# A 31-tap depthwise convolution split into even and odd tokens, with a new list schedule around it

## The chip, the core and the metric

The kernel runs on one core of one Trainium2 chip. The metric is the time of one execution of the program in microseconds (us) on the device. A second, profiled execution gives the trace that is read here; its span is the stretch from the first to the last instruction that the profiler records.

PE is TensorE (matmuls; PEld its weight loads), DVE is VectorE, ACT is ScalarE, POOL is GpSimd and SP is SyncE. POOL and SP do almost nothing here but issue transfers.

## What is computed

One layer of a hybrid decoder on 512 tokens of 1024 channels, in fp32. Cut to what matters:

```python
h = rmsnorm(x); proj = h @ w_in          # gb, gc, v | u, ug | q | three gates
y_a = (gb * conv3(gc * v)) @ w_a_out
u = u * sigmoid(ug)
u = causal_dwconv(u, conv_b_w) + conv_b_bias          # 31 taps, per channel
y_b = silu(layernorm(u)) @ w_b_out
y_c = cross_attention(q, mem) @ w_att_out
merged = sum(sigmoid(gate_i) * y_i)
x = x + merged @ w_o
x = x + (silu(conv3(h2 @ w_up)[gate]) * conv3(h2 @ w_up)[value]) @ w_down
out = rmsnorm(x)

def causal_dwconv(x, w):   # y[t] = sum_k w[k] * x[t - K + 1 + k]
```

The change touches the 31-tap convolution, `causal_dwconv(u, conv_b_w)`.

## The kernel before, in words

**Matmuls.** Every large product is taken in blocks ("quads") by a seven-product scheme of the Strassen kind, and each of the seven products is done three times, on a high and a low part of both operands (`multiply`, the matmuls of L681). One product of one quad, such as `(("mq", 1), 2)`, is 24 matmuls. Its weights come in as one 128x1024 tile from HBM; ACT casts the high part (`whi`, job `wh`, L500), DVE subtracts to get the low part (`wlo`, job `wl`, L504). For some products the low part is instead made by a negated copy on ACT (job `wn`, L519) and an accumulating transfer issued by POOL (L521). There are four buffers for such pairs, so a cast may run at most four products ahead of PE. Between a quad's products, partial sums are read from PSUM by ACT (jobs `r1`, `r5`, `r6`, `r4`: L708, L712, L723, L731) and DVE (`r2`, `r7`, `r3`: L457, L715).

**Stages by time.** PE does keys and values (to 60 us), the projections of `w_in` and the attention (60 to 440), the first output products (`merge`), the last gate, branch B's output product (quads `mq 0` and `mq 1`, 515 to 553), the merged product with `w_o` (stages `wo a` to `wo g`, 553 to 597), the up projection (597 to 835, eleven pairs of quads `up 0` to `up 10`), and the down projection to the end. The activations' combinations for branch B's quads (named `b00`, `b10`, `b11`, `t4` to `t7` after the seven products) are split into high (L1386, ACT) and low parts (L1391, DVE).

**The 31-tap convolution** (L1206 to L1267) runs on ACT and DVE alone. For each of four pairs `p` of 128-channel tiles (one 128x1024 tile: two tiles of 512 tokens) ACT writes the first product with the bias into a new tile `acc` (L1221, twice 128x512). Of the other 30 shifts, 23 are done as a product on ACT into a temporary `tp` (L1246, two instructions of 128 x (512 - s)) and an addition of both halves on DVE (L1253, one instruction); the seven shifts that are multiples of four are done on DVE alone by a multiply-add (L1238, two instructions). The four results are then summed and centred for the layer norm (`tot1`, `tot2`, `centre`, `lns`), and a swish is taken (L1344).

**Order.** PE's order is written out by hand (`QUAD_ORDER`, `WO`, `UP`, `DOWN`). Everything else is a job of class `Jobs` (L122 to L333): each job has an engine, an estimated cost, its predecessors and the tiles that it takes. The due time of a job is worked back from the PE product that needs it; then the scheduler repeatedly takes the job that can start first, and among those the one that is due first. Two tables bend this: `LATER` adds an offset to the due time of a kind of job, and `AHEAD` keeps a kind from starting more than so many us before it is due. `issue_in_program_order` then holds every engine to the order found, so an instruction that waits holds up all that stand behind it on its engine. Tiles live in rings (17 + 6 large places, 6 load buffers, 6 temporaries, 8 PSUM banks); a load waits until its place is free. The planner charges a fixed table cost to ACT only at the first sigmoid (`sg 0`), the exponentials, one later sigmoid and the first silu; the swish (L1344) and the second half of the gate's sigmoid (L1511) carry no such cost.

Of the kernel before, what the change touches and what calls it, by code (L numbers as in the profile page):

```python
# [10 lines left out]
AF = mybir.ActivationFunctionType  # L11
# [5 lines left out]
KC = D // P  # L17
# [54 lines left out]
LATER = {  # L72
    "ACT cf": 96, "ACT high": -211, "ACT kh": 28, "ACT oh": -43, "ACT qh": -31, "ACT r1 mq": -254,
# [3 lines left out]
    "DVE h2 t4": -36, "DVE kl": -6, "DVE kt": 11, "DVE mgl a": 32, "DVE mgl f": 25,  # L77
    "DVE ms d": 104, "DVE ptl": 21, "DVE ql": 99, "DVE r2 gate": 78, "DVE r2 up": 14,
    "DVE s6 glu": -67, "DVE tap 3": -4, "DVE tot1": -33, "DVE vl": 158, "DVE weigh": 139,
# [5 lines left out]
}  # L85

AHEAD = {
# [3 lines left out]
}  # L91


# [243 lines left out]
def hybrid_block_kernel(  # L337
# [64 lines left out]
    def two(key):  # L402

        return tiles[key].rearrange("p (c n) -> p c n", c=2)
# [34 lines left out]
    def par(key, i):  # L439
        return pk[:, cols[key] + i : cols[key] + i + 1]  # L440
# [544 lines left out]
    for p in range(4):  # L985
# [35 lines left out]
            use=[("x", p), ("rows", "x")] + (hb if p % 2 else []))  # L1021

    job(("ldp",), "SP", 0.3, lambda: nc.sync.dma_start(
        out=pk[:, N_GAINS:], in_=packed[:, N_GAINS:]), [("ldx", 3)], LOAD_LATENCY)
    scale_jobs("x", R_X, ("ss", "x"), NT)

    def pe_squares(s, key, n, width, after, total=1024):
# [175 lines left out]
               use=[("pth", h), ("ptl", h), ("vh", h // 2), ("vl", h // 2)], unit=False)  # L1203


    def by_act(p, s):  # L1206

        return s in ACT_TAPS

    for p in range(4):  # L1210
        job(("sg", p), "ACT", actv(1024) + (0 if p else TABLE), lambda p=p: nc.scalar.activation(
            tiles["ug", p], tiles["ug", p], AF.Sigmoid), ready_of(("glu", p), 0),
            use=[("ug", p)])
        job(("um", p), "DVE", dve(1024), lambda p=p: nc.vector.tensor_tensor(
            tiles["u", p], tiles["u", p], tiles["ug", p], op=ALU.mult),
            [("sg", p)] + ready_of(("glu", p), 1), use=[("ug", p), ("u", p)])

        def conv_start(p=p):
            make(("acc", p))
            for j in range(2):  # L1220
                nc.scalar.activation(  # L1221
                    two(("acc", p))[:, j, :], two(("u", p))[:, j, :], AF.Identity,
                    bias=par("conv_b_bias", 2 * p + j),
                    scale=par("conv_b_w", (K_B - 1) * KC + 2 * p + j),
                )

        job(("tap", p, 0), "ACT", 2 * scaled_act(512, 0.09), conv_start,
            [("um", p), ("ldp",)] + ([("tap", p - 1, K_B - 4)] if p else []),
            take=[(("acc", p), ANY)], use=[("u", p)])
        made_taps = []  # L1230
        for s in range(1, K_B):
            def weight(j, p=p, s=s):
                return par("conv_b_w", (K_B - 1 - s) * KC + 2 * p + j)

            def tap(p=p, s=s, weight=weight):
                for j in range(2):
                    a = two(("acc", p))[:, j, s:]
                    nc.vector.scalar_tensor_tensor(  # L1238
                        a, two(("u", p))[:, j, : SEQ - s], weight(j), a,
                        op0=ALU.mult, op1=ALU.add,  # L1240
                    )

            def tap_product(p=p, s=s, weight=weight):
                make(("tp", p, s))
                for j in range(2):
                    nc.scalar.activation(  # L1246
                        two(("tp", p, s))[:, j, s:], two(("u", p))[:, j, : SEQ - s], AF.Copy,
                        scale=weight(j),
                    )

            def tap_add(p=p, s=s):
                a = two(("acc", p))[:, :, s:]
                nc.vector.tensor_tensor(a, a, two(("tp", p, s))[:, :, s:], op=ALU.add)  # L1253

            if by_act(p, s):
                job(("tp", p, s), "ACT", 2 * scaled_act(512 - s), tap_product,
                    [("tap", p, 0), ("ldp",)] + made_taps[-2:-1], take=[(("tp", p, s), ANY)],
                    use=[("u", p)])
                job(("tap", p, s), "DVE", dve(1024 - 2 * s), tap_add,
                    [("tap", p, s - 1), ("tp", p, s)], use=[("acc", p), ("tp", p, s)])  # L1260
                made_taps.append(("tap", p, s))
            else:
                job(("tap", p, s), "DVE", 2 * TAP, tap, [("tap", p, s - 1), ("ldp",)],
                    use=[("acc", p), ("u", p)])


    conv_done = [("tap", p, K_B - 1) for p in range(4)]  # L1267

    def first_sum(key, a, b):
        make(key)  # L1270
# [6 lines left out]
    def sums_split(s, key):  # L1277
# [12 lines left out]
            use=[key])  # L1290
        job((s, "low"), "DVE", dve(512), low, [(s, "high")], use=[key, (s, "parts")])

    job("tot1", "DVE", dve(1024), lambda: first_sum(("tot",), ("acc", 0), ("acc", 1)),
        conv_done[:3], take=[(("tot",), ANY)], use=[("acc", 0), ("acc", 1)])
    job("tot2", "DVE", dve(1024), lambda: add_into(("tot",), ("acc", 2)), ["tot1", conv_done[2]],
        use=[("tot",), ("acc", 2)])
    job(("mu", "sum"), "DVE", dve(1024), lambda: add_into(("tot",), ("acc", 3)),
        ["tot2", conv_done[3]], use=[("tot",), ("acc", 3)])
    sums_split("mu", ("tot",))

    def channel_mean(s):
# [10 lines left out]
        return t.unsqueeze(1).broadcast_to([P, 2, SEQ])  # L1312

    for p in range(4):
        acc = ("acc", p)
        job(("centre", p), "DVE", dve(1024), lambda p=p: nc.vector.tensor_tensor(
            two(("acc", p)), two(("acc", p)), on_both(tiles["bank", "mu"]), op=ALU.subtract),
            [("mu", "mean")], use=[acc, ("bank", "mu")])

        def centre_square(p=p):  # L1320
            make(("csq", p))
            nc.scalar.activation(tiles["csq", p], tiles["acc", p], AF.Square)
# [10 lines left out]
    scale_jobs("v", R_V, ("ss", "v"), NT)  # L1333

    for p in range(4):
        acc = ("acc", p)
        job(("lns", p), "DVE", dve(1024), lambda p=p: nc.vector.tensor_tensor(
            two(("acc", p)), two(("acc", p)), on_both(tiles["rows", "v"]), op=ALU.mult),
            [("v", "rows")], use=[acc, ("rows", "v")])

        def swish(p=p):
            for j in range(2):
                t = two(("acc", p))[:, j, :]
# [22 lines left out]


    def rows_of(p, r):
        return two(("acc", p))[:, :, r * HALF : (r + 1) * HALF]

    def y_parts(key, e, src, after, use):
        last = next(f for f in OPERAND if OPERAND[f] == key)
# [26 lines left out]

    Y5 = ("y", "t5")  # L1400
    for e in range(2):
        top, end = ("acc", e), ("acc", 2 + e)
# [434 lines left out]
    for q in range(QUADS):  # L1837
# [5 lines left out]
        for value, src, acc in ((0, ("gt", q), ("gtc", q)), (1, ("uu", q), ("upc", q))):  # L1843
            conv3_jobs(
                ("cf", q, value), src, acc,
                lambda k, j, q=q, v=value: par(
                    "conv_ffn_w", k * 2 * FC + v * FC + 2 * q + j),
                ready_of(up, value) + ([("z", q - 1)] if q else []), "tm",
            )
        job(("silu", q), "ACT", actv(1024) + (0 if q else TABLE), lambda q=q: nc.scalar.activation(  # L1850
            tiles["gtc", q], tiles["gtc", q], AF.Silu), [(("cf", q, 0), "done")],
# [484 lines left out]
```

## Time and profile before

| | |
|---|---|
| median of 3 runs | 929.57 us (927.53 to 930.92) |
| profiled execution | 929.3 us, of it span 927.5 us |
| granted TensorE clock, mean | 0.997 |
| PE busy | 914.6 us (99%) |
| DVE busy | 852.0 us (92%) in 980 instructions |
| ACT busy | 685.2 us (74%) in 938 instructions |
| transfers | 196.91 MB, 212 GB/s on the mean |

A row of a view reads: line, engine, operation, output <- inputs, shapes, count, then busy time and mean length. An instruction's length overlaps a little with the next one's: neighbours of 128x1024 on DVE are 1.22 us long and start 1.14 us apart, on ACT 1.05 long and 0.95 apart. A row of waits reads: engine, line <- what it waited for: us in all, times, longest.

### The profile page before, as it was taken

The page shows a single profiled execution, that of the slowest core. Times are in us where ns is not written, and L with a number is a line of the kernel's source. Part 1 is how long each engine was busy: PE and PEld are TensorE (multiplying, and loading weights), DVE is VectorE, ACT ScalarE, POOL GpSimd, SP SyncE. Part 2 cuts the span into 40 slices and gives each one's busy share as a digit, 9 for nine tenths or more (in the row PEclk, how much of TensorE's full clock was granted, in tenths as well). Part 3 has the DMA queues.
Part 4 walks back from the last instruction along what each step waited for, and adds up shares of the span by engine and source line. Part 5 has one row for each costly group of instructions (what it writes and reads, how often), then busy time and mean ns, then how long its engine had stood idle before and what let it go on. Part 6 is the DMA issues. An engine that isn't in the chain of part 4 may idle for free.

```text
span 927.5 us, 17130 instructions
## 1 busy us (share of the span) xinstructions
PE 914.6 (99%) x6821; PEld 866.5 (93%) x6821; DVE 852.0 (92%) x980; ACT 685.2 (74%) x938; POOL 137.1 (15%) x165
## 2 busy tenths in 40 slices
PE   9999999999999999999999998999999999999997
PEld 8999999999989999999899996898999999988886
DVE  6897999999999999799996999996989889999977
ACT  7576988889997886678857973875766676765655
POOL 0021111100011211110110211121121121002300
PEclk9999999999999999999999999999999999999999
DMA  9999788745679888897857899999999677789972
GB/s 358 394 262 204 176 162 182 180 115 111 172 155 267 181 186 178 198 238 202 204 131 189 209 287 322 231 218 301 253 236 230 152 171 169 188 271 314 264 139 91
DMA packets 56097, 196.91 MB, mean 212 GB/s; under 512 B 6353, under 2 KB 6737, under 8 KB 56017
## 3 DMA queue, kind: packets, MB, share of 16 engines
q0 software_dynamic: 22608, 81.54, 48.9%
q1 hardware_dynamic: 33120, 114.02, 34.1%
q8 instruction: 53, 0.87, 0.4%
q10 hardware_dynamic: 288, 0.27, 0.1%
q14 instruction: 28, 0.22, 0.1%
HBM read 191.60 MB, written 4.19 MB: 211 GB/s over the span
## 4 chain that ended last, share of the span: by engine, by line
PE 91%; DVE 5%; DMA 3%; issue 1%; ACT 0%; SPq 0%; DVEq 0%; POOL 0%; POOLq 0%; ACTq 0%
PE bank L681 60%; PE bank L453 6%; PE bank L452 6%; PE bank L451 6%; PE bank L1486 3%; PE bank L1488 3%; PE bank L1487 3%; PE bank L937 2%; DMA ('up', 3)_966_7341<-in_w_up 2%; DVE wlo L504 1%; DMA y_sum<-in_w_down 1%; DVE mg L1562 1%; DVE mgl L1672 1%; PE bank L1864 0%; PE ss L810 0%
## 5 line engine op out<-in xcount | busy, mean ns | idle before, releaser
L500 ACT CAST whi<-wf 128x1024 fp32r<-128x1024 f32 x206 | 214.8, 1044 | 102.0 <-PE bank L681 53.5
L504 DVE TENSOR_TENSOR wlo<-wf,whi 128x1024 fp32r<-128x1024 f32 (+1 forms) x200 | 241.6, 1212 | 31.4 <-ACT whi L500 28.4
L1246 ACT ACTIVATE tp<-u,pk 128x482 f32<-128x482 f32 (+22 forms) x184 | 118.9, 704 | 4.2 <-DVE acc L1253 3.7
L1253 DVE TENSOR_TENSOR acc<-acc,tp 128x1022 f32<-128x1022 f32 (+22 forms) x92 | 109.2, 1188 | 4.0 <-ACT tp L1246 2.7
L638 POOL DMA_DIRECT2D wf<-in_w_in x50 | 44.2, 891 | 231.8 <-DVE wlo L504 185.7
L681 PE MATMUL bank<-ft6h,whi 128*128 128x256 f32 x248 | 69.4, 280 | 2.4 <-ACT gt L708 2.4
L681 PE MATMUL bank<-ft6h,wlo 128*128 128x256 f32 x248 | 69.4, 280 | 0.0
L681 PE MATMUL bank<-ft6l,whi 128*128 128x256 f32 x248 | 69.4, 280 | 0.0
L681 PE MATMUL bank<-fb11h,wlo 128*128 128x256 f32 x248 | 68.6, 277 | 0.5 <-DVE wlo L504 0.5
L681 PE MATMUL bank<-ft5h,whi 128*128 128x256 f32 x248 | 68.9, 278 | 0.0
L681 PE MATMUL bank<-ft5l,whi 128*128 128x256 f32 x248 | 68.8, 278 | 0.0
L681 PE MATMUL bank<-ft5h,wlo 128*128 128x256 f32 x248 | 68.8, 278 | 0.0
L681 PE MATMUL bank<-fb10h,whi 128*128 128x256 f32 x248 | 68.8, 278 | 0.0
L681 PE MATMUL bank<-fb00h,whi 128*128 128x256 f32 x248 | 68.8, 277 | 0.0
L681 PE MATMUL bank<-ft7h,whi 128*128 128x256 f32 x248 | 68.7, 277 | 0.0
L681 PE MATMUL bank<-ft7l,whi 128*128 128x256 f32 x248 | 68.7, 277 | 0.0
L681 PE MATMUL bank<-ft7h,wlo 128*128 128x256 f32 x248 | 68.7, 277 | 0.0
L681 PE MATMUL bank<-fb00l,whi 128*128 128x256 f32 x248 | 68.7, 277 | 0.0
L681 PE MATMUL bank<-fb00h,wlo 128*128 128x256 f32 x248 | 68.7, 277 | 0.0
L681 PE MATMUL bank<-fb11h,whi 128*128 128x256 f32 x248 | 68.7, 277 | 0.0
L681 PE MATMUL bank<-fb10h,wlo 128*128 128x256 f32 x248 | 68.6, 277 | 0.0
L681 PE MATMUL bank<-fb10l,whi 128*128 128x256 f32 x248 | 68.6, 277 | 0.0
(408 smaller groups left out, 3150.6 us busy)
## 6 DMA issues: line engine op xcount, KB each, us to landing
wf<-in_w_in SPq DMA_DIRECT2D x52, 512.0 KB, 5.3
wf<-in_w_in POOLq DMA_DIRECT2D x50, 512.0 KB, 6.7
wf<-in_w_up SPq DMA_DIRECT2D x31, 512.0 KB, 6.6
wf<-in_w_up POOLq DMA_DIRECT2D x30, 512.0 KB, 7.0
wf<-in_w_down SPq DMA_DIRECT2D x15, 512.0 KB, 4.1
wf<-in_w_att_out SPq DMA_DIRECT2D x8, 512.0 KB, 3.5
wf<-in_w_a_out SPq DMA_DIRECT2D x8, 512.0 KB, 4.5
wf<-in_w_b_out SPq DMA_DIRECT2D x8, 512.0 KB, 5.9
```

Of the source, the lines that this page charges most:

```text
L451: nc.tensor.matmul(ps, s_hi, w_hi, start=start, stop=False, skip_group_check=again)
L452: nc.tensor.matmul(ps, s_hi, w_lo, start=False, stop=False, skip_group_check=again)
L453: nc.tensor.matmul(ps, s_lo, w_hi, start=False, stop=stop, skip_group_check=again)
L500: nc.scalar.copy(parts[0], src())
L504: nc.vector.tensor_tensor(lo, src(), hi.bitcast(F32), op=ALU.subtract)
L638: nc.gpsimd.dma_start(out=tiles[key], in_=block(w, col[c], k), accum_op=ALU.add)
L681: nc.tensor.matmul(ps[:, c, :], w[:, k, at], a[k], start=first and n == 0, stop=i == 3 and n == 2, skip_group_check=again,)
L1246: nc.scalar.activation(two(("tp", p, s))[:, j, s:], two(("u", p))[:, j, : SEQ - s], AF.Copy, scale=weight(j),)
L1253: nc.vector.tensor_tensor(a, a, two(("tp", p, s))[:, :, s:], op=ALU.add)
L1486: nc.tensor.matmul(ps, w_hi[:, i, at], hi, start=first, stop=False)
L1487: nc.tensor.matmul(ps, w_hi[:, i, at], lo, start=False, stop=False)
L1488: nc.tensor.matmul(ps, w_lo[:, i, at], hi, start=False, stop=last)
```

## The change

The convolution is taken on even and odd tokens apart. With a sequence of 256 even and one of 256 odd tokens per tile, a 31-tap filter falls into 16 even and 15 odd taps, which would need four convolutions of half the length (each sort of token with each sort of tap). Three are made: even tokens with even-numbered taps and odd with odd (`ab`, four rows of 256), and the sum of even and odd tokens with the sums of neighbouring taps (`cc`); the last less the first two gives the mixed terms. The tokens are read in place with a step of two elements (`parity`).

- New on DVE: `taps` (sums of taps, once), `xsum2` (sum of even and odd tokens, one 128x512), `less`, `even`, `odd` (putting together, about 128x512 each), with strided reads in `xsum2` and strided writes in `even` and `odd`.
- On ACT, each pair `p` has 4 products to start `ab`, 50 products for its shifts 1 to 15 without 4 and 9, and 32 for `cc`: 86 products of 128 x (256 - s), 54 of them reading with the step of two.
- On DVE, shifts 4 and 9 of `ab` are done by four multiply-adds of 128 x (256 - s) each; the other shifts are 12 additions of 128 x 4 x (256 - s) and one of 128 x 2 x 241; `cc` takes 15 additions of 128 x 2 x (256 - s).
- The result goes back into `u`, so the tile `acc` is gone. The sums of taps take the place of `conv_ffn_w` in the packed parameters, whose load is split off as `ldf` behind `("less", 3)`; the FFN's convolution waits for it.
- `LATER` goes from 57 entries to 9, `AHEAD` from 14 to 4, and with them the order of all jobs on ACT, DVE, SP and POOL is found anew. PE's order is the same, instruction by instruction.

```diff
-ACT_TAPS = [s for s in range(1, 31) if s % 4]
+DVE_TAPS = (4, 9)
...
 LATER = {
-    "ACT cf": 96, "ACT high": -211, "ACT kh": 28, "ACT oh": -43, "ACT qh": -31, "ACT r1 mq": -254,
...
+    "DVE fl h2 t4": 7, "DVE fl h2 t7": 82, "DVE kt": 114, "DVE r7 up": -172, "DVE vl": 43,
+    "DVE wl mix 2": 4, "SP ld merge 0": -11, "SP ld up s": -15, "SP ld up v": -7,
 }
...
+        def parity(j, r, n=HALF, u=u):
+            return two(u)[:, j, r : r + 2 * n - 1 : 2]
+        def x_sum(u=u, cc=cc):
+            make(cc)
+            nc.vector.tensor_tensor(
+                four(cc)[:, 0:2, :], two(u)[:, :, 0::2], two(u)[:, :, 1::2], op=ALU.add)
...
+            def tap_product(s=s, tp=tp, d=d, parity=parity, weight=weight):
+                make(tp)
                 for j in range(2):
-                    nc.scalar.activation(
-                        two(("tp", p, s))[:, j, s:], two(("u", p))[:, j, : SEQ - s], AF.Copy,
-                        scale=weight(j),
-                    )
-            def tap_add(p=p, s=s):
-                a = two(("acc", p))[:, :, s:]
-                nc.vector.tensor_tensor(a, a, two(("tp", p, s))[:, :, s:], op=ALU.add)
+                    for r in range(1 if s == TAPS - 1 else 2):
+                        nc.scalar.activation(
+                            four(tp)[:, 2 * j + r, d:], parity(j, r, HALF - d), AF.Copy,
+                            scale=weight(s, j, r))
+            def tap_add(tp=tp, d=d, rows=rows, ab=ab):
+                a = four(ab)[:, rows, d:]
+                nc.vector.tensor_tensor(a, a, four(tp)[:, rows, d:], op=ALU.add)
...
+        def less_even(cc=cc, ab=ab):
+            c = four(cc)[:, 2:4, :]
+            nc.vector.tensor_tensor(c, c, four(ab)[:, 0::2, :], op=ALU.subtract)
+        def even_tokens(u=u, ab=ab):
+            a, b = four(ab)[:, 0::2, :], four(ab)[:, 1::2, :]
+            nc.vector.tensor_copy(two(u)[:, :, 0:1], a[:, :, 0:1])
+            nc.vector.tensor_tensor(
+                two(u)[:, :, 2::2], a[:, :, 1:], b[:, :, : HALF - 1], op=ALU.add)
+        def odd_tokens(u=u, ab=ab, cc=cc):
+            nc.vector.tensor_tensor(
+                two(u)[:, :, 1::2], four(cc)[:, 2:4, :], four(ab)[:, 1::2, :], op=ALU.subtract)
```

Three places of the new order are shown; line numbers of the changed kernel are its own (its L488 is L500 before, L492 is L504, L507 is L519, L1479 is L1391, L1755 is L1667, L1938 is L1850).

The first is DVE in branch B's quads (about 523 to 531 us of the trace before). A row `wlo` is the low part of a weight tile. Before, `wlo_6189` is that of product 2 of `mq 1`, `wlo_6222` that of product 6 of `mq 0`; `ft7l` and `ft6l` are low parts of branch B's activations:

```order
L1521 TENSOR_TENSOR g_4970<-bank_5896,g_4970 128x512
L504 TENSOR_TENSOR wlo_6189<-wf_5956,whi_6188 128x1024
L1391 TENSOR_TENSOR ft7l_6152<-acc_2344,ft7h_6151 128x512
L504 TENSOR_TENSOR wlo_6222<-wf_5777,whi_6221 128x1024
L457 SCALAR_TENSOR_TENSOR acc_1146<-acc_1146 128x2x256
L457 SCALAR_TENSOR_TENSOR acc_2344<-acc_2344 128x2x256
L457 SCALAR_TENSOR_TENSOR acc_3233<-acc_1146,acc_3233 128x2x256
L504 TENSOR_TENSOR wlo_6264<-wf_5880,whi_6263 128x1024
L1391 TENSOR_TENSOR ft6l_6269<-acc_1146,ft6h_6268 128x512
```

In the changed kernel `wlo_6309` is that of product 2 of `mq 0`, `wlo_6387` that of product 6 of `mq 0`, and `wlo_6351` that of product 2 of `mq 1`:

```order
L445 SCALAR_TENSOR_TENSOR u_757<-u_757 128x2x256
L492 TENSOR_TENSOR wlo_6309<-wf_6092,whi_6308 128x1024
L445 SCALAR_TENSOR_TENSOR u_893<-u_893 128x2x256
L492 TENSOR_TENSOR wlo_6387<-wf_5944,whi_6386 128x1024
L1479 TENSOR_TENSOR ft6l_6393<-u_757,ft6h_6392 128x512
L1479 TENSOR_TENSOR ft6l_6393<-u_893,ft6h_6392 128x512
L492 TENSOR_TENSOR wlo_6351<-wf_6123,whi_6350 128x1024
L492 TENSOR_TENSOR wlo_6436<-wf_6047,whi_6435 128x1024
L703 TENSOR_TENSOR y_6313<-y_6313,bank_6400 128x2x256
```

The low part for product 2 of `mq 1` moved behind that for product 6 of `mq 0` and behind both low parts of `ft6`; PE still takes product 2 of `mq 1` first.

The second is ACT ahead of the stage `wo` (about 541 to 552 us). L519 (L507) is the negated copy after which POOL issues the accumulating transfer; `whoh` and `whol` are the halves of `w_o`'s own tiles, `mgh` is the high part of the merged activations. Before:

```order
L500 CAST whoh_6443<-wf_6339 128x1024
L519 ACTIVATE whol_6444<-wf_6339 128x1024
L500 CAST whi_6476<-wf_5880 128x1024
L500 CAST whoh_6484<-wf_6377 128x1024
L1667 CAST mgh_6489<-mg_6480 128x512
L519 ACTIVATE whol_6485<-wf_6377 128x1024
L500 CAST whoh_6518<-wf_6413 128x1024
L1667 CAST mgh_6527<-mg_6516 128x512
L519 ACTIVATE whol_6519<-wf_6413 128x1024
L500 CAST whoh_6556<-wf_6447 128x1024
L1667 CAST mgh_6489<-mg_6480 128x512
L519 ACTIVATE whol_6557<-wf_6447 128x1024
```

In the changed kernel:

```order
L488 CAST whi_6606<-wf_5944 128x1024
L488 CAST whoh_6611<-wf_6532 128x1024
L507 ACTIVATE whol_6612<-wf_6532 128x1024
L488 CAST whi_6645<-wf_6047 128x1024
L1755 CAST mgh_6650<-mg_6643 128x512
L488 CAST whoh_6655<-wo_6433 128x1024
L488 CAST whoh_6683<-wf_6577 128x1024
L488 CAST whi_6687<-wo_6346 128x1024
L507 ACTIVATE whol_6684<-wf_6577 128x1024
L488 CAST whoh_6723<-wf_6614 128x1024
L1755 CAST mgh_6650<-mg_6643 128x512
L507 ACTIVATE whol_6724<-wf_6614 128x1024
```

Ahead of the second negated copy (`whol_6485` before, `whol_6684` now) stand two more casts, `whoh_6655` and `whi_6687`, of tiles that were cast behind the fourth negated copy before. POOL issues the four transfers in the same order in both.

The third is ACT in the up projection (about 645 to 652 us), around the first silu. L708 (L696) is the first read of quad `up 2` from PSUM, for which PE waits; `whi_7581` (`whi_7744` now) is the cast for product 7 of `up 2`, and L731 (L719) the last read of `up 1`. Before:

```order
L500 CAST whi_7537<-('up', 3)_966_7341 128x1024
L1850 ACT_TABLE_LOAD
L1850 ACTIVATE gtc_7475<-gtc_7475 128x1024
L500 CAST whi_7572<-wf_7236 128x1024
L731 ACTIVATE uu_7408<-bank_7042 128x2x256
L708 COPY gt_7579<-bank_7123 128x2x256
L500 CAST whi_7581<-wf_6937 128x1024
L500 CAST whi_7611<-('up', 3)_977_7439 128x1024
```

In the changed kernel:

```order
L488 CAST whi_7704<-('up', 3)_963_7510 128x1024
L1938 ACT_TABLE_LOAD
L1938 ACTIVATE gtc_7642<-gtc_7642 128x1024
L488 CAST whi_7737<-wf_7435 128x1024
L488 CAST whi_7744<-wf_7147 128x1024
L696 COPY gt_7748<-bank_7302 128x2x256
L719 ACTIVATE uu_7437<-bank_7205 128x2x256
L488 CAST whi_7776<-('up', 3)_974_7610 128x1024
```

The cast for product 7 moved ahead of that first read, and the last read of `up 1` behind it.

More of the change, by code (lines that the diff above doesn't have):

```diff
@@ L1267, in hybrid_block_kernel @@
-    conv_done = [("tap", p, K_B - 1) for p in range(4)]
+        u, ab, cc = ("u", p), ("ab", p), ("cc", p)
+        def parity(j, r, n=HALF, u=u):
[4 more added lines that the diff above has]
+                four(cc)[:, 0:2, :], two(u)[:, :, 0::2], two(u)[:, :, 1::2], op=ALU.add)
+        job(("xsum2", p), "DVE", dve(512), x_sum, [("um", p)] + ([("less", p - 1)] if p else []), take=[(cc, ANY)], use=[u])
@@ new lines, in sums_product, with sums_start @@
+        def sums_product(out, row, i, p=p, cc=cc):
+            for j in range(2):
+                at = (TAPS - 1) * KC + 2 * p + j
+                more = {"bias": tap_sums[:, at : at + 1]} if i == 0 else {}
+                nc.scalar.activation(
+                    four(out)[:, row + j, i:], four(cc)[:, j, : HALF - i],
+                    AF.Copy if i else AF.Identity, scale=sum_of_taps(i, 2 * p + j), **more)
+        def sums_start(cc=cc, sums_product=sums_product):
+            sums_product(cc, 2, 0)
@@ L1269, in first_sum @@
+        job(("less", p), "DVE", dve(512), less_even, [last[cc], last[ab]], use=[cc, ab])
+        job(("even", p), "DVE", dve(512) + 0.1, even_tokens, [last[ab], last[cc]], use=[u, ab])
+        job(("odd", p), "DVE", dve(512), odd_tokens, [("less", p), ("even", p)],
+            use=[u, ab, cc])
+    conv_done = [("odd", p) for p in range(4)]
     def first_sum(key, a, b):
@@ L1342, in swish @@
             for j in range(2):
[L1343 removed]
+                t = two(("u", p))[:, j, :]
                 nc.scalar.activation(
```

143 lines of the change are left out of this document (93 added, 50 removed), and 11 rows, old and new, of tables (AHEAD, LATER).

## The prediction, made before the changed kernel was run

> **What bounds the kernel now.** First the page: busy time of each engine, and the chain that ended last.
>
> ```profile
> PE 914.6 (99%) x6821; PEld 866.5 (93%) x6821; DVE 852.0 (92%) x980; ACT 685.2 (74%) x938; POOL 137.1 (15%) x165
> PE 91%; DVE 5%; DMA 3%; issue 1%; ACT 0%; SPq 0%; DVEq 0%; POOL 0%; POOLq 0%; ACTq 0%
> ```
>
> PE is busy 914.6 of 927.5 us and makes 91% of the chain. Its order is the same after the change, so its own work is a constant, and a gain can come only from its waits. The view of PE's waits lists them all:
>
> ```profile
> PE bank L681 <- ACT gt L708: 2.4, 1, 2.4
> PE bank L452 <- DMA whol<-in_w_o: 2.2, 2, 1.5
> PE bank L1864 <- POOL ident masks.py:199: 1.4, 1, 1.4
> PE bank L681 <- DVE wlo L504: 0.5, 1, 0.5
> PE bank L452 <- DVE wlo L504: 0.4, 1, 0.4
> PE bank L453 <- DVE zl L2028: 0.3, 1, 0.3
> ```
>
> That is 7.2 us, of which the 1.4 at the start stays. None names the convolution (L1221 to L1253). Third, busy time by stretch, to see which engines have room where (stretch; its length; PE, PEld, DVE, ACT, POOL busy; granted clock, DMA share, GB/s):
>
> ```profile
> 100.00:230.00 130.00, 130.00 (x1089) 128.10 (x1088) 126.05 (x160) 114.92 (x186) 16.44 (x19) 1.00 0.71 156
> 230.00:285.00 55.00, 55.00 (x297) 47.63 (x296) 53.66 (x58) 47.69 (x70) 6.07 (x7) 1.00 0.72 178
> 285.00:390.00 105.00, 105.00 (x919) 104.88 (x918) 98.49 (x105) 79.11 (x107) 18.20 (x21) 1.00 0.86 197
> 460.00:508.00 48.00, 48.00 (x325) 44.24 (x324) 40.30 (x43) 30.35 (x39) 4.32 (x5) 1.00 0.73 171
> 508.00:534.00 26.00, 26.00 (x223) 25.65 (x222) 24.94 (x33) 25.29 (x38) 6.96 (x8) 1.00 0.83 190
> 534.00:573.00 39.00, 36.77 (x243) 32.47 (x242) 38.97 (x52) 23.62 (x28) 5.17 (x6) 1.00 1.04 308
> 652.00:654.00 2.00, 2.00 (x12) 2.00 (x11) 2.00 (x3) 1.81 (x4) 0.00 (x0) 0.50 1.11 262
> 654.00:656.00 2.00, 2.00 (x14) 2.00 (x14) 1.97 (x3) 1.36 (x2) 1.75 (x2) 0.71 1.06 229
> ```
>
> From 100 to 390 us, where most of the convolution runs, PE never waits. DVE is the fuller of the two there: 278.20 busy of 290, ACT 241.72. PE first loses time in 534 to 573, when DVE is busy 38.97 of 39 and the DMA engines are full. Between the two lies 460 to 508, where DVE is busy only 40.30 of 48 and PE all the time: whatever lead DVE has won by then ends as idle time, since its next work needs PE's results. The last two rows belong to the wait of 2.4 us near 650: behind it the clock stood at 0.50 and 0.71 for 2 us each, which cost 1.00 + 0.58 = 1.6 us more. So without any wait but the first the profiled run would take 929.3 - (7.2 - 1.4) - 1.6 = 921.9 us, the floor for this PE order.
>
> **The convolution itself.** The rows of the old parts, and the nearest rows for the new lengths:
>
> ```profile
> L1246 ACT ACTIVATE tp<-u,pk 128x482 f32<-128x482 f32 (+22 forms) x184 | 118.9, 704 | 4.2 <-DVE acc L1253 3.7
> L1253 DVE TENSOR_TENSOR acc<-acc,tp 128x1022 f32<-128x1022 f32 (+22 forms) x92 | 109.2, 1188 | 4.0 <-ACT tp L1246 2.7
> L1238 DVE SCALAR_TENSOR_TENSOR acc<-u,pk,acc x56: 711/731/746, 104.1 to 460.6; 128x508 f32<-128x508 f32 x8, 128x504 f32<-128x504 f32 x8, 128x500 f32<-128x500 f32 x8, 128x496 f32<-128x496 f32 x8
> L1221 ACT ACTIVATE acc<-u,pk x8: 799/808/880, 91.5 to 334.2; 128x512 f32<-128x512 f32 x8
> L773 ACT ACTIVATE mh<-mem,pk x8: 492/502/509, 3.7 to 15.5; 128x256 fp32r<-128x256 f32 x8
> L1009 DVE SCALAR_TENSOR_TENSOR hb<-x,pk,rows x16: 473/473/481, 32.8 to 38.7; 128x256 f32<-128x256 f32 x16
> L1391 DVE TENSOR_TENSOR fb10l<-acc,fb10h x2: 684/685/686, 517.8 to 518.4; 128x512 fp32r<-128x512 f32 x2
> ```
>
> Neighbours overlap: a DVE row counts for about 0.08 us less than its length, an ACT row for 0.10 less. Before, DVE: 92 x 1.11 + 56 x 0.65 = 138.5 us; ACT: 184 x 0.60 + 8 x 0.71 = 116 us. After, on DVE per pair: 12 additions of nearly 128x1024 at 1.11 (13.3), 16 of about 128x512 at 0.59 (9.4), eight multiply-adds of 128x256 at 0.39 (3.1), and `xsum2`, `less`, `even`, `odd` (2.5): 28.3, times four 113. So **DVE saves 25 us**. On ACT, 86 products of 128x256 at 0.40 make 34.4 per pair, 138 in all: **ACT gets 22 us more**, since shorter products pay the fixed part more often.
>
> Neither number enters the sum: up to 480 us PE waits for neither engine, and DVE's lead ends in the idle time of 460 to 508. What hides ACT's share is its idle time, 48.3 us in 100 to 390. By counting, on ACT's new order, the work ahead of each weight cast, ACT carries 6 us more than before at 100 us and 43 more at 390, because the taps are also done sooner; 37 of the 48.3 us are used up. That is thin cover.
>
> No row shows an operand with a step of two. A strided product of 256 costs at least the 0.40 of L773; if each element took two places, it would cost the 0.60 of a product of twice the length (L1246). I take 0.40, as the count of elements is 256, and keep 0.60 for a rival. The Trainium skill ("SBUF — State Buffer", section on Door 1, in its note on cachelines) says that SBUF has lines of 16 bytes and that two hits on a line are enough for full speed; a step of two fp32 elements gives just two, so by that page the stride is free and the sum the same. No run here shows it yet.
>
> Edits with one answer, all at nothing: `taps` and `ldf` (a short sum, and a small load long before the FFN's convolution at 635 us); the place `acc` that is no longer taken (loads wait for DVE and PE, not for room, where PE waits); the order up to 508 us, in which the low parts lie at most a few us later than before, inside the slack.
>
> **The new order from 508 us** is what counts. *Branch B.* The stretch of 524 to 529 us, DVE, ACT and PE:
>
> ```profile
> 520.72 0.68 DVE L1391 TENSOR_TENSOR ft7l<-acc,ft7h 128x512 fp32r<-128x512 f32 x1
> 521.32 0.68 DVE L1416 TENSOR_TENSOR acc<-acc,acc 128x512 f32<-128x512 f32 x1
> 524.68 1.23 DVE L504 TENSOR_TENSOR wlo<-wf,whi 128x1024 fp32r<-128x1024 f32 x1 [0.87 <-ACT whi L500]
> 525.07 1.05 ACT L500 CAST whi<-wf 128x1024 fp32r<-128x1024 f32 x1
> 526.43 1.22 DVE L504 TENSOR_TENSOR wlo<-wf,whi 128x1024 fp32r<-128x1024 f32 x1
> 528.41 0.28 PE L681 MATMUL bank<-fb10h,whi 128*128 128x256 f32 x1
> ```
>
> The low part of product 2 of `mq 1` ran at 524.68, and PE takes it from 528.4. Now it stands behind that of product 6 of `mq 0`, whose cast ends at 526.1 (the ACT row; ACT has the same amount ahead of it), and behind two parts `ft6l` of 0.60 each (the distance of the first two rows). So it ends at 526.1 + 1.14 + 1.20 + 1.22 = 529.6: a new wait of **1.2 us**. Behind it on DVE stand the low parts that PE needs from 531 on, all with the same delay, which PE now shares.
>
> *Stage `wo`.* The last of POOL's four transfers, the ACT copies ahead of the second and fourth, and the time to land:
>
> ```profile
> 546.64 1.06 ACT L519 ACTIVATE whol<-wf 128x1024 fp32r<-128x1024 f32 x1
> 551.47 1.06 ACT L519 ACTIVATE whol<-wf 128x1024 fp32r<-128x1024 f32 x1
> 552.83 0.86 POOL L521 DMA_DIRECT2D whol<-in_w_o  x1 [1.55 <-ACT whol L519]
> DMA to landing us min/median/max: 8.3/9.2/11.9
> ```
>
> PE's wait of 1.5 us ended with the landing at 552.83 + 11.9 = 564.7. In the new order two more casts of 0.95 stand ahead of the second copy, and ACT waits for activations that are 1.2 later: the fourth transfer is issued about 3.1 later, at 555.9, and lands between 564.2 and 567.8. Against 564.7 PE's slip is then anything from -0.3 (the whole first wait absorbed) to +3.1. Since the queue is as full as before I take a landing near the late end, 566.9: slip **+2.2**, the 1.2 from above included. A wait beyond 2.4 us may also lower the clock as at 650 (1.6 us). The Trainium skill ("TensorE: Matmul & The Clock Gate", Part 1) says that the clock falls after an idle window of about 3.4 us; by that none of these waits would lower it, but the rows of 652 to 656 disagree, as 2.4 us were enough. By the page the sum is the same, and only the upper end is lower by 1.6.
>
> *Up projection.* ACT before the wait of 2.4 us:
>
> ```profile
> 649.13 0.59 ACT L731 ACTIVATE uu<-bank 128x512 f32<-128x512 f32 x1
> 649.62 0.58 ACT L708 COPY gt<-bank 128x512 f32<-128x512 f32 x1
> 650.08 1.06 ACT L500 CAST whi<-wf 128x1024 fp32r<-128x1024 f32 x1
> ```
>
> PE waits for the L708 copy. Ahead of it now stands the cast (0.95) in place of the L731 read (0.49): **+0.5 us** (nothing, if the cast's wait is shared; 0.5 at most). The transfers ahead of it stay full, so I keep the rest of that wait.
>
> Sum: 2.2 + 0.5 = 2.7, and 929.3 + 2.7 = **932.0 us** (own range 929 to 936: the landing early or late, and the clock). The profiled run lies 0.3 below the median of 929.57, so the same sum on the median is 932.3. A measurement tells a difference from about 0.3% (2.8 us) on; 932.0 is at that edge.
>
> **Rivals.**
> - *The waits go* (faster). Loads of `w_o` and of `up 3` are reordered on SP; if they land a few us sooner, the waits for `whol` (2.2), for the low part (0.4), and for the L708 copy with its clock (2.4 + 1.6) vanish: 929.3 - 6.6 = 922.7. For it: `wo y 0` is loaded earlier and DVE has less to do. Against it: DVE's relief is spent before 508 us, and the DMA share of 1.04 leaves no room. It decides if the fourth transfer lands before PE asks, about 563.2.
> - *Nothing moves*: each new wait falls into an old one, 929.3.
> - *ACT overruns* (slower). 216 of its products are strided. At 0.60 each costs 0.20 more; the three and a half pairs done by 390 us have 189, so 38 us against 48.3 - 37 = 11 of idle: 27 us late, 956. It starts to bite from 0.06 us more per product. For it: the thin cover; against it: no more elements are handled.
> - *The change saves no DVE time*: if DVE's strided sums cost double (about 2 us per pair), 17 of the 25 us stay; with the limits above this changes nothing, so it is within the second rival.
>
> **How the numbers follow.** Forecast 0.42, waits go 0.28, nothing moves 0.10, ACT overruns 0.20. Of the forecast's own range a quarter (0.10) lies within 2.8 us of the median. Faster 0.28, same 0.10 + 0.10 = 0.20, slower 0.32 + 0.20 = 0.52. The range must reach both ways: 923 leaves out the best of the first rival, 946 the worse half of the last.
>
> **What would show it.** PE's waits should name DVE `wlo` near 528 with about 1.2 us, `whol` near 565 with 1 to 3, and the L708 copy near 652 with about 2.9; DVE busy near 827, ACT near 707; ACT products of 128x256 at 0.50 long. Wrong would be a wait of PE between 100 and 480, strided products over 0.56 long, or no wait at `whol`.

## The result, and the profile after

| | before | changed |
|---|---|---|
| median of 18 runs each | 928.56 us (926.76 to 930.93) | 931.10 us (929.50 to 932.95) |
| ratio, with 95% interval | | 1.0026 (1.0016 to 1.0036) |
| profiled execution, span | 929.3, 927.5 us | 929.75, 928.0 us |
| last matmul ends | 921.8 us | 921.8 us |

The changed kernel is slower by 0.26%, about 2.5 us: its interval leaves out 1, but it is below the 0.3% that were called the edge. 932.0 was forecast, 931.10 measured. The two profiled executions are only 0.45 us apart, and that has to be explained too.

The page of the changed kernel, busy times and chain:

```profile
PE 913.4 (98%) x6821; PEld 864.7 (93%) x6821; DVE 828.8 (89%) x998; ACT 706.2 (76%) x1090; POOL 137.3 (15%) x165
PE 80%; DMA 7%; DVE 6%; ACT 5%; issue 2%; SPq 0%; DVEq 0%; ACTq 0%; POOLq 0%
```

DVE lost 23 us of work and ACT gained 21; 827 and 707 were forecast. PE's work is the same, so the waits decide again. All waits of PE:

```profile
PE bank L440 <- DMA whol<-in_w_o: 1.9, 3, 0.9
PE bank L1952 <- POOL ident masks.py:199: 1.4, 1, 1.4
PE bank L669 <- DVE B L445: 1.3, 1, 1.3
PE bank L669 <- ACT gt L696: 1.2, 1, 1.2
PE bank L669 <- DVE wlo L492: 0.9, 1, 0.9
PE bank L441 <- DVE ql L1061: 0.6, 1, 0.6
PE bank L1841 <- DVE cols L1832: 0.4, 1, 0.4
PE bank L669 <- DVE V L445: 0.3, 1, 0.3
PE bank L925 <- DVE wlo L873: 0.2, 1, 0.2
```

The row `wlo` L492 is the wait that was forecast for branch B (1.2; here 0.9, at 533). `whol` did not grow. New are three rows that no step of the prediction had: `ql` near 167, `V` near 375 and `B` near 396, all inside the convolution's stretch; a fourth is `cols` near 606. The stretches, in the columns used before:

```profile
100.00:230.00 130.00, 129.40 (x1082) 127.30 (x1081) 127.82 (x176) 129.17 (x256) 18.73 (x22) 1.00 0.73 161
230.00:285.00 55.00, 55.00 (x301) 47.85 (x300) 43.93 (x57) 51.71 (x103) 5.19 (x6) 1.00 0.72 177
285.00:390.00 105.00, 104.67 (x908) 104.15 (x907) 102.00 (x119) 97.28 (x177) 16.50 (x20) 1.00 0.82 194
390.00:460.00 70.00, 68.66 (x526) 65.45 (x526) 51.44 (x58) 41.99 (x52) 11.26 (x13) 1.00 0.90 221
460.00:508.00 48.00, 48.00 (x324) 44.27 (x323) 31.77 (x33) 24.00 (x28) 5.19 (x6) 1.00 0.69 163
534.00:573.00 39.00, 37.09 (x265) 33.65 (x264) 39.00 (x53) 25.27 (x31) 7.84 (x9) 1.00 1.04 296
```

DVE is busier than before in 285 to 390 (102.00 against 98.49), although it has less to do in all, and much idler in 460 to 508 (31.77 of 48 against 40.30). Before, 390 to 460 was nearly full as well:

```profile
390.00:460.00 70.00, 70.00 (x525) 66.37 (x525) 67.27 (x71) 58.97 (x82) 10.38 (x12) 1.00 0.87 216
```

The new order does the taps sooner. The last instruction of the convolution starts at 409, where before it was 464. Between 390 and 508 DVE now has 24 us less to do: the saved time lies idle in front of branch B, as forecast, and the crowding comes earlier. On ACT it is close: 129.17 of 130 us are busy in 100 to 230, and of its 48.3 us of idle time in 100 to 390 there are 11.8 left, as the prediction had counted.

What PE loses per stage can be summed: the excess of the distance from one matmul's start to the next over the usual distance for its shape, wherever it is above 0.06 us, from 60 us on. Two executions of before and two of the changed order (the second of each is described below):

| lost us, in | before | before, again | changed | changed, held fixed |
|---|---|---|---|---|
| up to 508 us | 0.5 | 0.5 | 3.6 | 3.6 |
| branch B, 508 to 550 | 0.2 | 0.2 | 1.2 | 1.2 |
| `wo`, 550 to 597 | 4.0 | 5.0 | 3.0 | 3.0 |
| 597 to 640 | 0.2 | 0.2 | 0.9 | 1.0 |
| 640 to 670 | 5.2 | 2.4 | 1.5 | 3.0 |
| later | 0.5 | 0.5 | 0.1 | 0.1 |
| sum | 10.6 | 8.8 | 10.3 | 11.8 |

In these pairs the rows up to 550 repeat to 0.1 us; those where the data comes through full DMA queues do not. The early rows vary too, though: the execution of experiment 3, whose order is the same up to 508, lost 4.0 us there, and those of experiments 10 and 11, of one order up to there, 3.1 and 2.0. (The sums leave out the start and all smaller excesses, so they differ from the spans by up to 1 us.)

### The profile page after: what moved, and what is told of

It is laid out like the page before. It is cut to its first block, busy times and chain, and to the rows that moved or that the text cites. A ratio compares the mean times of both kernels' runs of the same rounds, so it can differ in the third digit from the quotient of the medians.

```text
span 928.0 us, 17335 instructions
## 1 busy us (share of the span) xinstructions
PE 913.4 (98%) x6821; PEld 864.7 (93%) x6821; DVE 828.8 (89%) x998; ACT 706.2 (76%) x1090; POOL 137.3 (15%) x165
## 4 chain that ended last, share of the span: by engine, by line
PE 80%; DMA 7%; DVE 6%; ACT 5%; issue 2%; SPq 0%; DVEq 0%; ACTq 0%; POOLq 0%
PE bank L669 49%; PE bank L441 6%; PE bank L440 6%; PE bank L439 6%; PE bank L1574 3%; PE bank L1576 3%; PE bank L1575 3%; DVE wlo L492 3%; DMA wf<-in_w_up 3%; PE bank L925 2%; DMA wf<-in_w_in 2%; ACT whi L488 1%; DMA whol<-in_w_o 1%; DMA wf<-in_w_o 1%; DVE ab L1298 1%
## 5 line engine op out<-in xcount | busy, mean ns | idle before, releaser
L488 ACT CAST whi<-wf 128x1024 fp32r<-128x1024 f32 x206 | 216.1, 1052 | 99.8 <-PE bank L669 36.1
L492 DVE TENSOR_TENSOR wlo<-wf,whi 128x1024 fp32r<-128x1024 f32 x200 | 241.5, 1213 | 42.7 <-ACT whi L488 42.3
L1292 ACT ACTIVATE tp<-u,pk 128x255 f32<-128x255 f32 (+12 forms) x200 | 89.3, 544 | 2.6 <-DVE cc L1309 1.6
L626 POOL DMA_DIRECT2D wf<-in_w_in x53 | 46.5, 887 | 255.8 <-DVE wlo L492 195.3
L669 PE MATMUL bank<-fb11l,whi 128*128 128x256 f32 x248 | 68.5, 276 | 0.0
```

What stands on the lines that cost most here:

```text
L488: nc.scalar.copy(parts[0], src())
L492: nc.vector.tensor_tensor(lo, src(), hi.bitcast(F32), op=ALU.subtract)
L626: nc.gpsimd.dma_start(out=tiles[key], in_=block(w, col[c], k), accum_op=ALU.add)
L669: nc.tensor.matmul(ps[:, c, :], w[:, k, at], a[k], start=first and n == 0, stop=i == 3 and n == 2, skip_group_check=again,)
L1292: nc.scalar.activation(four(tp)[:, 2 * j + r, d:], parity(j, r, HALF - d), AF.Copy, scale=weight(s, j, r))
```

## The experiments

**Theory A**: the loss is the sum of waits set by the new order, above all ahead of 400 and at 533, and PE keeps what it would win there. **Rival B**: waits swap for one another, because the transfers of `w_o` and `up 3` land when the queue has come to them; undoing one place wins nothing. A third question was whether the step of two costs anything. All ratios are to the kernel before, on the same chip.

**1. Before once more.** No edit.

> The kernel before, unchanged, for a second profile. Theory A (the wait of 2.4 us near 650 and the clock of 0.50 behind it belong to the order of before): they show again, within 0.3 us, and the median ratio is 1.000. Theory B (that wait hangs on when transfers land and differs from execution to execution): the wait near 650 comes out at least 0.8 us shorter or longer, with or without the lower clock, while the waits in 556 to 574 stay near 2.6 us.

Ratio 1.0008 (0.9993 to 1.0022), span 926.1. The waits that ended the profile of before now read:

```profile
PE bank L452 <- DMA whol<-in_w_o: 2.9, 3, 1.3
PE bank L681 <- ACT gt L708: 2.1, 1, 2.1
```

and the stretch behind the second:

```profile
652.00:654.00 2.00, 2.00 (x20) 2.00 (x20) 2.00 (x2) 2.00 (x5) 0.00 (x0) 1.00 1.06 270
```

The wait is of the order of before (2.1 against 2.4), as A had it, but the clock of 0.50 behind it need not come: here it is 1.00. So the first profile of before held 1.6 us that this one does not have, most of the difference between 0.45 us (one profile against one) and 2.5 us (18 runs against 18). It is not rare, though. Of the 103 executions of before whose mean clock is on record, 21 show 0.996 or less and take 930.1 us on the mean, the other 82 take 928.3; of the changed order it is 1 in 30. Where the clock fell in those is not recorded.

**2. The changed order held fixed.** The order that the scheduler finds is kept as a list, so that a single instruction can be moved without a new plan for the rest.

> The changed kernel with its order held fixed by a list, so that single instructions can be moved in the next runs: the same instructions on every engine. Expected ratio to before 1.0026 (1.0015 to 1.0037). Theory A (the waits are those of the order): waits of PE at about 0.6 near 167, 1.3 near 396, 0.9 near 533 and 1.2 near 652 show again within 0.3 us. Theory B (they are chance): some of them are gone and others have come.

Ratio 1.0039 (1.0025 to 1.0053), which overlaps the 1.0026 of the result. Waits at 167, 375, 396 and 533 are the same; of the 1.2 near 652 only 0.2 is left, a wait of 1.2 for a cast came near 645, and 640 to 670 lost 3.0 in place of 1.5 us, so there Theory B holds. Experiments 3 to 6 and 9 to 12 start from this kernel.

**3. Branch B's low part back in its old place.**

```diff
+MOVES = [(("wl", (("mq", 1), 2)), ("wl", (("mq", 0), 6)))]   # the first goes ahead of the second
```

> The changed kernel with one edit: the low part of product 2 of mq 1 ahead of that of product 6 of mq 0, as before the change. Theory A (the wait near 533 is made by that place, and PE keeps what it wins): the wait is gone and the time falls by 1.1 us, ratio to before about 1.0014. Theory B (the slip is given back at the transfers of w_o, which land when the DMA queue has come to them): the wait near 533 goes, the waits for whol grow by the same 1.1 us, and the time stays at 1.0026.

Ratio 1.0033 (1.0020 to 1.0046). PE's waits:

```profile
PE bank L693 <- ACT gt L720: 2.0, 1, 2.0
PE bank L464 <- DMA whol<-in_w_o: 1.8, 1, 1.8
PE bank L693 <- DVE B L469: 1.3, 1, 1.3
```

The wait at 533 is gone: the mechanism and its size (loss in branch B 1.2 to 0.2 us) are shown. But stage `wo` lost 4.0 in place of 3.0 us in this execution, the same 1 us. That is not B's mechanism as it was written: the waits for `whol` are 1.8 in place of 1.6 us. The rest is a lowered clock behind the wait of 1.8, which no profile of the unmoved order has there:

```profile
564.00:566.00 2.00, 2.00 (x6) 1.59 (x5) 2.00 (x3) 1.04 (x1) 0.00 (x0) 0.50 1.00 305
```

Nor did `w_o` come sooner: SP issued its first load at 537.33, in the fixed order at 536.45 (SP waits there for DVE's `wlo`, and one of these now waits 1.0 us for its cast). The 12 executions lie 1.3 us below those of the fixed order in the same batch (931.33 and 932.67), as A had it, but the two intervals overlap. So it is not settled whether PE keeps this microsecond.

**4. Two reads ahead of the taps' additions and of the short convolution.**

```diff
+MOVES = [(("r7", ("cv", 3)), ("tap", 3, 22)), (("r7", ("bb", 1)), (("c3", 3), 0, 1))]
```

> The changed kernel with two edits: on DVE the reads r7 of cv 3 and of bb 1 go ahead of an addition of the taps and of the short convolution's multiply-adds. Theory A (PE's waits near 375 and 396 come from DVE's order, and PE keeps what it wins): both are gone, 2.0 us less, ratio to before about 1.0004. Theory B (later waits swallow it, above all whol, whose data lands by the queue): the two waits go, but the waits for whol and the one near 652 grow by 1 us or more, and the ratio stays above 1.0015.

Ratio 1.0011 (0.9998 to 1.0024), 0.0028 below the fixed order in the same batch; span 926.6. The rows `B L445` and `V L445` are gone; two of 0.3 and 0.4 for reads on ACT took their place (loss up to 508 us: 3.6 to 2.6), and the loss near 640 to 670 was 1.5 where the fixed order had 3.0. The waits for `whol` stayed at 1.6. A is borne out for the early waits, at 1 us by the trace; whether the rest of the gain belongs to it or to chance near 650 the profiles can't tell, since that stage differs by as much between two executions of one order.

What held `B` up is to be read on DVE in the changed kernel, just before PE's wait ends at 395.9:

```profile
391.31 1.22 DVE L492 TENSOR_TENSOR wlo<-wf,whi 128x1024 fp32r<-128x1024 f32 x1
392.45 1.53 DVE L1530 SCALAR_TENSOR_TENSOR ya<-C,pk,ya 128x511 f32<-128x511 f32 x2
393.89 1.22 DVE L492 TENSOR_TENSOR wlo<-wf,whi 128x1024 fp32r<-128x1024 f32 x1
395.03 0.69 DVE L445 SCALAR_TENSOR_TENSOR B<-bank,B 128x512 f32<-128x512 f32 x1
```

PE's product that L445 reads ended near 391.8; the read could have gone at 392.5 and stands behind 2.6 us of other work. Before, the same read stood sooner, and PE took the next product into that bank at 392.43, 1.5 us after its end:

```profile
390.27 0.68 DVE L457 SCALAR_TENSOR_TENSOR B<-bank,B 128x512 f32<-128x512 f32 x1
392.43 0.28 PE L681 MATMUL bank<-ft4h,whi 128*128 128x256 f32 x1
```

**5. and 6. The step of the strided reads**: one, and four elements, in place of two. The edit is in `parity`, so it reaches the products on ACT and the multiply-adds on DVE; `xsum2` keeps its step of two. The taps then meet wrong tokens; count and order of instructions are the same.

```diff
-            return two(u)[:, j, r : r + 2 * n - 1 : 2]
+            return two(u)[:, j, r : r + n]                       # step one
+            return tiles[u][:, j : j + 4 * n - 3 : 4]            # step four
```

> The changed kernel, order held fixed, with the tokens of all strided reads taken from 256 neighbouring elements in place of every second one, on ACT and DVE (the taps then meet the wrong tokens, which is the part of the computation that changes). Theory A (the step of two costs little: products start 0.425 us apart with it, 0.39 without): the 200 products into tp get shorter by some 0.03 us, ACT loses about 6 us of busy time, and the time falls by 0 to 1 us (ratio to before 1.002 to 1.003). Theory B (the stride is what fills ACT and makes the waits near 167, 375 and 396): those waits go and the time falls by 2.5 us or more, ratio 1.000.

> The changed kernel, order held fixed, with every strided read taking every fourth element (wrong tokens again, as many elements). Theory A (two hits on a line of 16 bytes are needed, as the Trainium skill says on its page SBUF — State Buffer; a step of four fp32 gives one): products into tp become longer, at least 0.6 us in place of 0.53, ACT gains 20 us or more of busy time, and PE waits for it between 100 and 400, ratio to before above 1.01. Theory B (only the count of elements matters): lengths as with a step of two, ratio 1.0026 within 0.0015.

Step one: 1.0017 (1.0005 to 1.0029). Step four: 1.0478 (1.0455 to 1.0502), where Theory A holds. The products on ACT and the multiply-adds on DVE (minimum/median/maximum ns) with steps of two (the changed kernel):

```profile
L1292 ACT ACTIVATE tp<-u,pk x200: 493/530/628, 90.3 to 387.8; 128x255 f32<-128x255 f32 x8, 128x254 f32<-128x254 f32 x8, 128x253 f32<-128x253 f32 x8, 128x251 f32<-128x251 f32 x8
L1315 DVE SCALAR_TENSOR_TENSOR ab<-u,pk,ab x32: 470/473/479, 105.2 to 358.9; 128x252 f32<-128x252 f32 x16, 128x247 f32<-128x247 f32 x16
```

of one:

```profile
L1315 ACT ACTIVATE tp<-u,pk x200: 481/497/560, 90.5 to 387.4; 128x255 f32<-128x255 f32 x8, 128x254 f32<-128x254 f32 x8, 128x253 f32<-128x253 f32 x8, 128x251 f32<-128x251 f32 x8
L1338 DVE SCALAR_TENSOR_TENSOR ab<-u,pk,ab x32: 470/473/479, 105.3 to 358.2; 128x252 f32<-128x252 f32 x16, 128x247 f32<-128x247 f32 x16
```

and of four:

```profile
L1315 ACT ACTIVATE tp<-u,pk x200: 705/747/831, 91.1 to 429.7; 128x255 f32<-128x255 f32 x8, 128x254 f32<-128x254 f32 x8, 128x253 f32<-128x253 f32 x8, 128x251 f32<-128x251 f32 x8
L1338 DVE SCALAR_TENSOR_TENSOR ab<-u,pk,ab x32: 651/664/678, 108.7 to 399.7; 128x252 f32<-128x252 f32 x16, 128x247 f32<-128x247 f32 x16
```

A step of two costs DVE nothing and ACT 0.03 us of 0.50; a step of four costs 0.19 and 0.25. The Trainium skill ("SBUF — State Buffer", section on Door 1) has a rule that fits: two accesses to a line of 16 bytes are needed for full speed. These rows agree on DVE at steps of two and four; the 0.03 us on ACT at a step of two are beside it. That note of the Trainium skill also calls a distance of 4 fp32 free, which the rows of step four do not bear out. With step one the waits near 167 and 375 leave the view (by the distances of PE's matmuls, 0.3 of 0.7 us stay at 167), that for `B` stays at 1.4: ACT's extra 4 us (706.2 against 702.0 busy) are behind the first two, DVE's order behind the third. The time agrees with Theory A, and its interval overlaps that of the unmoved order, so the stride's share of the loss is not clear of noise. The run with step four is the prediction's rival "ACT overruns" made real: 0.22 us more than with a step of two on 216 products is 47 us, ACT is busy 752.9 us, and PE waits for its reads,

```profile
PE bank L692 <- ACT C L734: 15.8, 3, 9.0
PE bank L692 <- ACT ug L734: 5.0, 2, 2.9
```

and the time grows by about 42 us (1.0478 against 1.0026). Not all of that is waiting for ACT: behind three of the waits the clock stood near 0.5 for 6.8 us, which cost about 10 us,

```profile
131.30:138.10 6.80, 5.75 (x27) 5.75 (x28) 6.45 (x10) 6.80 (x12) 0.86 (x1) 0.52 0.52 80
319.00:325.80 6.80, 2.75 (x13) 2.75 (x14) 5.63 (x7) 6.80 (x13) 1.75 (x2) 0.52 0.55 161
346.30:353.10 6.80, 4.87 (x23) 4.87 (x24) 5.74 (x6) 6.47 (x11) 0.86 (x1) 0.52 0.61 127
```

and DVE's 32 multiply-adds took 6 us more as well. The cover was indeed thin.

**7. and 8. Convolution and tables apart.**

```diff
 # the old convolution with the tables of the changed kernel; the new one with those of before
-LATER = {...}
+LATER = {...}   # the other kernel's, and AHEAD with it
```

> The kernel before with the two tables of due times of the changed kernel: the old convolution under the new rules. Theory A (the order loses the time from 508 us on, ACT's added work only the waits before 400): waits near 533 and for whol as after the change, none near 375 and 396, ratio to before about 1.001. Theory B (the tables alone are the loss): 1.0026 or more. Theory C (the tables fit only the new convolution): new waits of several us in the convolution's stretch, above 1.005.

> The changed kernel with the two tables of before: the new convolution under the old rules. Theory A (order and convolution each bring waits of their own): waits between 100 and 400 remain, the one near 533 does not, ratio 1.001 to 1.004. Theory B (the new convolution by itself gains, and the new tables give it away): ratio below 1.000. Theory C (the old tables fit only the old convolution): several us of new waits, ratio above 1.005.

The old convolution with the new tables: 1.0082 (1.0063 to 1.0101); the new one with the old tables: 1.0351 (1.0329 to 1.0372). The largest wait of each:

```profile
PE bank L1475 <- DVE yal L1346: 5.6, 1, 5.6
```

```profile
PE bank L681 <- ACT g L708: 24.4, 1, 24.4
```

Theory C holds for both: neither table fits the other job list. (Of the first kernel's 8 us about 5 are a clock of 0.5 behind its waits of 5.6 and 2.8 us.) In the second, ACT's read `g` stands at 449.3 behind products of the taps, which wait in turn for additions on DVE. So the loss can't be split into a part of the convolution and a part of the tables; only the places of single instructions can be priced.

**9. The casts ahead of `w_o`'s transfers moved back.**

```diff
+MOVES = [(("wh", ("wo", "f", 0)), ("wh", ("wo", "f", 1))), (("wh", ("wo", "d", 0)), ("wh", ("wo", "f", 1))),
+         (("wl", ("wo", "f", 0)), ("ms", "f"))]
```

> The changed kernel, order held fixed, with the two extra casts (and the low part that follows one of them) moved back behind the fourth negated copy, as before the change. Theory A (those casts delay POOL's transfers, as the prediction had it): the four transfers are issued 1 to 3 us earlier, the waits for whol fall from about 1.6 to below 0.5 us, and the time by about 1 us, ratio about 1.002. Theory B (the landing hangs on the full DMA queue, not on the issue): the transfers are issued earlier but land no earlier, the waits for whol stay at 1.3 us or more, ratio 1.0026 to 1.004.

Ratio 1.0041 (1.0027 to 1.0054): no gain is seen. The fourth transfer's issue in the changed kernel and here (in brackets, the idle time before it and what ended it):

```profile
558.30 0.86 POOL L509 DMA_DIRECT2D whol<-in_w_o  x1 [1.55 <-ACT whol L507]
```

```profile
557.88 0.86 POOL L535 DMA_DIRECT2D whol<-in_w_o  x1 [1.56 <-ACT whol L533]
```

It came only 0.4 us sooner, but not because the casts are free. From the first transfer's issue to the second it was 5.3 us (548.20 to 553.46) and is 3.9 (549.17 to 553.05): the casts cost 1.4 of the 1.9 us that I counted. In this execution `w_o`'s first tile landed later, ahead of any moved instruction, and ACT waited for it:

```profile
545.89 1.05 ACT L488 CAST whoh<-wf 128x1024 fp32r<-128x1024 f32 x1 [0.66 <-DMA wf<-in_w_o]
546.87 1.05 ACT L514 CAST whoh<-wf 128x1024 fp32r<-128x1024 f32 x1 [1.82 <-DMA wf<-in_w_o]
```

So this run alone does not settle A against B. The next ones say more.

**10. to 12. All places together.** Seven places (those of 3 and 4, two more reads of `bb 1`, the scaled x near 606, the first read of `up 2`); then with those of 9; then with two additions of stage `d` as well.

> The changed kernel with seven instructions moved: the four reads of the gate B quad near 375 to 396 (r7 of cv 3 and bb 1, r1 and r6 of bb 1), the low part of product 2 of mq 1, the scaled x near 606, and the first read of up 2 near 652. Theory A (PE keeps what it wins early): the waits before 400 other than that near 167 are gone, with that near 533, 3 to 4 us in all; of it up to 1.5 is given back at whol; the ratio to before is 0.999 to 1.001. Theory B (each gain is swallowed by the next transfer): ratio 1.002 or more, with waits for whol above 3 us or a wait near 650 above 2.5.

> As the last one, with the casts ahead of w_o's transfers moved back as well. Theory A (issue sets the landing): whol's waits below 1 us and a ratio of 0.998 to 1.000, at or below before. Theory B (the queue sets it): no faster than the last one, within 0.0015.

> The run before with nine and one more pair of places: the additions x1 of stage d go back ahead of the low parts mgl g and of wo g 0 on DVE, as before the change, since PE waited 0.9 us for the scaled x near 592. Theory A (what is won there is kept): that wait goes, 0.7 us less, ratio to before 0.999 to 1.001. Theory B (the first reads of the up projection behind it, whose weights come by the full DMA queue, swallow it): waits between 597 and 660 grow by as much and the ratio stays at 1.001. In neither does the new convolution beat the old one by more than 0.2 per cent.

Ratios 1.0017 (1.0003 to 1.0031), 1.0008 (0.9993 to 1.0022) and 1.0003 (0.9990 to 1.0017). From the first to the second the fourth transfer is issued 2.0 us sooner (557.47 to 555.46), and the waits for `whol` stay (1.7 and 1.8), as B had it; the gain of 0.0009 is within the intervals. The last one's span is 925.6, its longest waits besides the first:

```profile
PE bank L704 <- DVE y L480: 1.1, 1, 1.1
PE bank L475 <- DMA whol<-in_w_o: 1.1, 2, 0.7
PE bank L476 <- DVE ql L1096: 0.6, 1, 0.6
```

Twelve moved instructions undo the loss; the new convolution then ties with the old, and the 23 us that DVE saves buy nothing. No version beats before clear of its interval. What each move is worth alone is shown only where a wait goes and its stage loses less: at 375, 396 and 533. The wait for `ql` near 167 was left: moving it ahead of the taps would need another place in the ring of tiles, which wasn't tried.

## Why the prediction was right, and which steps were not

The time came out near the sum, but partly by luck: of the sum's three terms one was found.

- **What bounds it**: right. PE's work stayed (914.6 and 913.4 busy), and time followed its waits.
- **The convolution's sums**: right. DVE -23 against -25 us, ACT +21 against +22, and ACT's idle time used up as counted. The stride was taken as free; it costs ACT 0.03 us per product, 4 us of busy time in all.
- **"Neither number enters the sum: up to 480 us PE waits for neither engine"**: wrong, and this is the failed step; a wait of PE between 100 and 480 was among the prediction's own signs of being wrong. PE lost 3.6 us there against 0.5. The rival "ACT overruns" had the place and the thin cover, but was priced only from 0.06 us per product on. I had walked the low parts of the weights in that stretch, which ended 4 to 6 us before PE took them, and not the reads from PSUM, whose slack was far smaller (that of `B` ended 1.5 us before); DVE was held to be relieved, while the new order crowds it (102.00 of 105 us).
- **Branch B**, 1.2 us: right in mechanism and size (1.1 lost at 533, 0.2 in the whole stage when the place is undone).
- **Stage `wo`**, +1.0 us: wrong. The loss fell (3.0 against 4.0 and 5.0). The fourth transfer was issued 5.5 us later than before (558.30 against 552.83), not 3.1: 4.1 is what PE was late by then (3.1 up to 508, 1.0 in branch B), 1.4 the casts. That PE's waits shrank fits its coming so late itself; the sum had allowed for such absorbing only at its lower end, -0.3.
- **Up projection**, +0.5 us: not seen. 1.5 and 3.0 lost in two executions of the changed order, 2.4 to 5.2 in two of before; the stage varies more than the term. The 0.7 us more from 597 to 640 (`cols` among it) were in no term.
- **The clock behind 650** was put into the base as a property of the kernel; one execution of before has it and another has not. With the second profile of before the base is lower by that 1.6 us. No wait of the changed kernel's own profile up to the last matmul was followed by a lower clock; one of 1.8 us in experiment 3 was.

So the sum came out near the truth by luck: an overlooked 3 us stood for two terms that weren't there. Forecast 2.7 us over the profile; measured 2.5 over the median. That those early waits reach the time, experiment 4 shows in part: two moved reads gave back 1 us by the trace and 2.7 by the medians, and where the other 1.7 came from stays open.

## What to carry to other kernels

Here, where one engine is busy 98% of the time, work taken off the others bought nothing by itself. In such a kernel each place where the busy engine hands over (reads from PSUM most of all) has to be walked in the new order, because the slack there was the smallest in this one. A wait removed ahead of a stage that is fed by full DMA queues may only move there; these runs leave that open. And one profile is one execution: take a second before a wait on the DMA path or a lowered clock goes into a sum.

## What the runs showed of the hardware beyond the forecast

- A step of four fp32 elements in SBUF costs some 50% on ACT (747 against 497 ns for 250 elements) and 40% on DVE (664 against 473); a step of two 7% on ACT and nothing on DVE, where sums of 128x512 with a step of two on one side took 684 to 688 ns in the median, a contiguous one 685 (`fb10l`, L1391 before).
- A wait of PE of 2.4 us was followed by a clock of 0.50 and 0.71 for 4 us in one execution; one of 2.1 us at the same place in another was followed by none. In experiment 3 a wait of 1.8 us near 562 was followed by 0.50 (564 to 566), one of 2.0 us near 653 by none. What decides it these runs do not show.
